# Down projection as seven half-size products over pairs of inner tiles, its operands staged in DRAM, with ScalarE's and VectorE's order written out by hand

## The chip, the cores and the metric

The kernel runs on one core of a Trainium2 chip. The metric is the device time of one execution in microseconds (us). Engines are named as in the profile: PE is TensorE's matmul, PEld its weight load, ACT ScalarE, DVE VectorE, POOL GpSimd, SP SyncE, which here only issues DMAs.

## What is computed

One step of an encoder layer over 640 tokens (512 of a prompt, 128 of running streams), model width 2048, inner width 5632, in fp32:

```python
def layer(x, lp, states):
...
    x = x + jnp.concatenate([y_a, y_b, y_c, y_d], axis=-1) @ w_out

    h = rmsnorm(x, g_ffn)
    gt, new_hist_f = causal_dwconv(h @ w_ffn_gate, ffn_conv_w, hist_f)
    x = x + (jax.nn.silu(gt) * (h @ w_ffn_up)) @ w_ffn_down
```

The four parts `y_a` to `y_d` (short convolution, gated linear attention, long convolution, banded attention) and the projections around them come first; the change touches what follows them, the last three lines. A final norm ends the step.

## The kernel before, in words

Activations lie transposed: features on the 128 partitions, the T = 640 tokens along the free axis, in two halves of H = 320. Width 2048 is KT = 16 tiles, the inner width NF = 44 tiles. An fp32 product is made of three matmuls in the reduced format fp32r: each operand is split into a high part (`hi`, a copy by ACT, L115) and a low part (`lo`, the difference, by DVE, L119), and hi·hi, hi·lo and lo·hi are added in PSUM. Weights come by SP's queue into `raw` (`wraw`, L101, three buffers) and are split by `wsplit` (L107). PE's order is the program's; DVE's and ACT's are set by a scheduler, with `high_priority` for some instructions.

**Gate and up** (L895 to L1013). A block of 256 inner columns by 2048 rows is one group `g` of 22, done first for the gate weights and then for the up weights. `seven` (L908) forms from the four blocks a11, a12, a21, a22 of the weights (each 128 x 1024) and from seven operand combinations `ops[0..6]` of the normed input, made once before, seven products of half size instead of eight: `product` (L895) is 8 x 3 = 24 matmuls of 128 weights by 320 columns. Sums of weight blocks are DVE adds of 128 x 1024 (L917, L923, L924, L929). `snap` (L903) copies a PSUM sum to SBUF on ACT, `put` (L946) combines a second sum with it on DVE. Gate results `fu` get the norm factor (L986, L987), the convolution of width 3 (L994 to L996) and a Silu (L998) to become `fc`; up results `ft` get the norm factor and are multiplied by `fc` (L1010 to L1012); POOL stores each inner tile `ft` to `td` in DRAM (L1013). POOL also copies the convolution's history to `hist` (L989, L990).

**Down projection** (L1016 to L1063). `act` (L1019) loads an inner tile of `td` to `ta` by SP and splits it. Five chunks of eight inner tiles follow: for each of the 16 output tiles, weights of 128 x 1024 are loaded (L1039, four rows of 1024 bytes per partition) and split, 48 matmuls run (`mm3`, L125), and DVE adds the sum to `acc` (L1046), which starts as the residual, read from `x1d`. The next chunk's inner tiles are loaded meanwhile. Inner tiles 40 and 41 follow with 192 matmuls, adds at L1060.

**Tail** (L1066 on). The last two inner tiles (weights `wl`), the final norm and the outputs.

A few lines say what the words can't:

```python
def mm3(ps, w, k, x, start, stop, m=P, halves=(0, 1)):
...
    for i, (a, j) in enumerate(((hi, 0), (hi, 1), (lo, 0))):
        for h in halves:
            PE.matmul(ps[:m, h, :H], a[:, k * m:(k + 1) * m], x[j][:, h * H:(h + 1) * H],
                      start=start and i == 0, stop=stop and i == 2)
```

## Time and profile before

| | us |
|---|---|
| median of 3 runs | 2719.23 |
| lowest run | 2717.56 |
| the profiled execution | 2721.07 |
| its span in the profile | 2719.3 |
| busy: PE | 2680.3 |
| busy: DVE | 1578.2 |
| busy: ACT | 913.2 |
| busy: POOL | 241.3 |

The profile shows one execution; times in it run from the span's start. Up to about 982 us the mixers and projections run, up to about 2067 gate and up, up to about 2671 the down projection, then the tail. Busy shares are averages over these stages. A row that counts matmuls gives their time in sequence on the chain of waits, while a row of one matmul gives its full length, of which the next one covers a part.

### The profile page before, as it was taken

The numbers are of one execution on the slowest core, as the hardware profiler recorded it, in microseconds if no ns is written. First come the engines' busy times: TensorE is split into PE (matmuls) and PEld (weight loads), VectorE is DVE, ScalarE is ACT, GpSimd is POOL, SyncE is SP. The second block draws the span as 40 slices with busy tenths as digits, with TensorE's granted clock in tenths as the row PEclk, the third lists the DMA queues.
The fourth block names the chain that finished last, engine by engine and source line by source line (L and its number), as shares of the span: only waits on it lengthen the run. The fifth ranks groups of instructions, "written<-read, shape, count | busy, mean of one in ns | idle before, by whom it ended". The sixth has DMA issues, their size and how long they took to land.

```text
span 2719.3 us, 42977 instructions
## 1 busy us (share of the span) xinstructions
PE 2680.3 (99%) x18156; PEld 2616.5 (96%) x18156; DVE 1578.2 (58%) x2248; ACT 913.2 (34%) x1243; POOL 241.3 (9%) x397
## 2 busy tenths in 40 slices
PE   8999999999999989999999999999999999999998
PEld 8988898999999989999999999999998999999997
DVE  6877434253533467777777877777776233242236
ACT  5113434331332344344444434434444122121113
POOL 0012110000000011111111111111111000000002
PEclk9999999999999989999999999999999999999999
DMA  6334332222243323333233233332237233232223
GB/s 217 89 111 127 108 94 66 83 72 63 78 133 119 112 76 99 108 98 101 94 102 111 91 100 100 105 99 94 97 113 256 75 112 113 78 104 78 73 76 117
DMA packets 118969, 281.42 MB, mean 103 GB/s; under 512 B 11192, under 2 KB 58968, under 8 KB 118776
## 3 DMA queue, kind: packets, MB, share of 16 engines
q1 hardware_dynamic: 107544, 241.26, 27.9%
q0 software_dynamic: 11088, 37.41, 4.2%
q8 instruction: 142, 2.33, 0.4%
q14 instruction: 51, 0.42, 0.1%
q10 hardware_dynamic: 144, 0.01, 0.0%
HBM read 248.93 MB, written 32.46 MB: 103 GB/s over the span
## 4 chain that ended last, share of the span: by engine, by line
PE 90%; issue 6%; DVE 2%; ACT 1%; DMA 1%; POOL 0%; SPq 0%; ACTq 0%; POOLq 0%; DVEq 0%
PE main L130 42%; PE b L900 40%; PE main L157 3%; PE m L157 1%; PE main L1083 1%; PE m L463 1%; PE m L442 1%; PE m L476 0%; DMA ta<-td 0%; PE main L745 0%; PE m L210 0%; DMA raw<-in_w_in 0%; PE m L199 0%; DVE lo L119 0%; DVE sq L226 0%
## 5 line engine op out<-in xcount | busy, mean ns | idle before, releaser
L130 PE MATMUL main<-o,hi 128*128 128x320 f32 x5888 | 1116.8, 312 | 13.2 <-ACT o L219 6.4
L900 PE MATMUL b<-op,hi 128*128 128x320 f32 x4928 | 1085.8, 309 | 11.0 <-ACT hi L115 9.8
L130 PEld LDWEIGHTS main<-o,hi 128*128 128x128 f32 x5888 | 926.4, 189 | 26.7 <-issue 7.4
L900 PEld LDWEIGHTS b<-op,hi 128*128 128x128 f32 x4928 | 825.5, 188 | 12.0 <-ACT hi L115 10.1
L900 PE MATMUL b<-op,lo 128*128 128x320 f32 x2464 | 762.6, 309 | 0.7 <-DVE lo L119 0.7
L115 ACT ACTIVATE hi<-raw 128x1024 fp32r<-128x1024 f32 (+1 forms) x337 | 356.3, 1057 | 1157.8 <-PE main L130 817.1
L130 PE MATMUL main<-o,lo 128*128 128x320 f32 x2944 | 674.2, 310 | 0.8 <-DVE lo L119 0.8
L119 DVE TENSOR_TENSOR lo<-raw,hi 128x1024 fp32r<-128x1024 f32 (+1 forms) x337 | 411.6, 1222 | 322.3 <-ACT hi L115 317.5
L130 PEld LDWEIGHTS main<-o,lo 128*128 128x128 f32 x2944 | 494.4, 189 | 1.3 <-DVE lo L119 1.3
L900 PEld LDWEIGHTS b<-op,lo 128*128 128x128 f32 x2464 | 463.6, 188 | 1.3 <-DVE lo L119 1.3
L1046 DVE TENSOR_TENSOR acc<-acc,main 128x640 f32<-128x640 f32 x80 | 65.7, 822 | 371.8 <-PE main L130 371.8
L119 DVE TENSOR_TENSOR lo<-x,hi 128x1024 fp32r<-128x1024 f32 x132 | 161.6, 1225 | 104.8 <-ACT hi L115 99.9
L115 ACT ACTIVATE hi<-x 128x1024 fp32r<-128x1024 f32 x132 | 139.9, 1060 | 224.7 <-PE b L900 214.1
L119 DVE TENSOR_TENSOR lo<-a,hi 128x1024 fp32r<-128x1024 f32 x44 | 54.0, 1227 | 97.8 <-ACT hi L115 97.8
L905 ACT ACTIVATE sn<-b 128x320 f32<-128x320 f32 x176 | 74.6, 424 | 92.1 <-PE b L900 92.1
L989 POOL COPY hist<-fu 128x2 f32<-128x2 f32 x44 | 79.5, 1806 | 119.0 <-DVE fu L986 118.8
L346 DVE SCALAR_TENSOR_TENSOR cc<-gp,pb,cc 128x512 f32<-128x512 f32 x120 | 89.7, 747 | 0.0
L157 PE MATMUL main<-hi,o 128*128 128x512 f32 x256 | 84.6, 391 | 0.0
L996 DVE SCALAR_TENSOR_TENSOR fc<-fu,pb,fc 128x656 f32<-128x656 f32 x88 | 79.0, 898 | 0.7
L115 ACT ACTIVATE hi<-a 128x1024 fp32r<-128x1024 f32 x44 | 46.6, 1060 | 79.7 <-PE b L900 46.8
L1013 POOL DMA_DIRECT2D td<-ft x44 | 23.8, 541 | 454.9 <-DVE ft L1012 437.1
L990 POOL COPY hist<-fu 128x16 f32<-128x16 f32 x44 | 31.1, 707 | 354.8 <-DVE fu L987 354.8
(291 smaller groups left out, 1804.0 us busy)
## 6 DMA issues: line engine op xcount, KB each, us to landing
raw<-in_w_d SPq DMA_DIRECT2D x88, 512.0 KB, 3.7
raw<-in_w_in SPq DMA_DIRECT2D x71, 512.0 KB, 3.8
raw<-in_w_g SPq DMA_DIRECT2D x66, 512.0 KB, 3.7
raw<-in_w_u SPq DMA_DIRECT2D x66, 512.0 KB, 3.9
td<-ft POOLq DMA_DIRECT2D x44, 320.0 KB, 2.5
ta<-td SPq DMA_DIRECT2D x44, 320.0 KB, 4.9
raw<-in_w_out SPq DMA_DIRECT2D x24, 512.0 KB, 3.8
a<-in_w_g SPq DMA_DIRECT2D x22, 512.0 KB, 3.7
```

The source lines that it names most:

```text
L115: S.activation(hi[:, c], raw[:, c], AF.Copy)
L119: latest[0] = V.tensor_sub(lo[:, c], raw[:, c], hi[:, c].bitcast(F32)).ins
L130: PE.matmul(ps[:m, h, :H], a[:, k * m:(k + 1) * m], x[j][:, h * H:(h + 1) * H], start=start and i == 0, stop=stop and i == 2)
L157: PE.matmul(pss[t], opnd[kt][j][:, t * P:(t + 1) * P], w[:, k * 512:(k + 1) * 512], start=(kt == 0 and i == 0), stop=(kt == KT - 1 and i = ...
L346: V.scalar_tensor_tensor(c[:, :512], gp[:, j:j + 512], w(j), c[:, :512], op0=ALU.mult, op1=ALU.add)
L442: PE.transpose(pp[:, t, :], p[:, t * P:(t + 1) * P], ident)
L900: PE.matmul(ps, a[:, kt * P:(kt + 1) * P], o[:, j, kt % 2], start=(start and kt == 0 and i == 0), stop=(kt == 7 and i == 2), skip_group_ch ...
L905: S.activation(t, ps, AF.Copy)
L989: G.tensor_copy(hist[:, k, 0:2], u[:, 512:514])
L990: G.tensor_copy(hist[:, k, 2:].rearrange("p (b t) -> p b t", b=NB), su(u)[:, :, 16:])
L996: V.scalar_tensor_tensor(c[:, :n], u[:, q:q + n], w[:, q:q + 1], c[:, :n], op0=ALU.mult, op1=ALU.add)
L1046: V.tensor_add(v2(acc[c]), v2(acc[c]), ps[:, :, :H])
```

## The change

The stages up to the output projection keep PE's order. In gate/up PE's products stay the same, 308 of 24 matmuls. What changes:

- ACT's and DVE's order is by hand: `run(q)` is one product slot. It issues ACT's high part of product q + 1, the product's matmuls, the lists `fronts` and `mids` of slot q, DVE's low part of q + 1, then the lists `sums` and `backs`. `after`, `put_in` and a table put work into these lists. `snap` is gone: `seed` copies a sum straight to its place in `fu` or `ft`, and `put` adds there.
- `stage` takes the two inner tiles of a group (a pair) and makes the seven operands of the down projection: four combinations by DVE and, for all seven, a high part by ACT and a low part by DVE, each then stored by POOL's queue to `od` in DRAM (320 KB a store). Pairs are made of inner tiles 4 to 41, 19 pairs. Inner tiles 0 to 3, 42 and 43 are only split and stored to `sd`.
- The down projection has a plain phase, inner tiles 0 to 3 for 16 output tiles, and then 32 steps. A step takes two output tiles (m of 8) and a run of pairs (four rounds, widths from `BOUNDS`), and makes seven products of width x 3 matmuls. Weights come by SP in rows of 512 bytes, a block per tag and one buffer each, their sums `x1`, `x2` are DVE adds, and `gather` adds each product's sum to `acc`.
- Pairs come back from `od` by POOL's queue (`fetch_pair`, three loads of 640 KB and one of 320 KB). Seven stay in SBUF; the next is fetched when the steps that are left no longer need the oldest. The residual comes by ACT's queue.
- The weights' pools move to the other side of SBUF; the tail's own are opened after the steps.

```diff
+od = drp.tile([19, P, 7, 2, H], F32, name="od")
+sd = drp.tile([6, P, 2, T], F32, name="sd")
...
-def seven(src, after=()):
-    after = dict(after)
-    a11, a21, a22 = wraw(src[0][:, :1024]), wraw(src[1][:, :1024]), wraw(src[1][:, 1024:])
-    with tc.high_priority():
-        a12 = gw.tile([P, 1024], F32, tag="r2", name=nm("a12"))
-        Y.dma_start(a12, src[0][:, 1024:])
-        x = gw.tile([P, 1024], F32, tag="xs", name=nm("x"))
-        V.tensor_add(x, a21, a22)
-    a, c, e, d = (bank8()[:, :H] for _ in range(4))
-    product(0, a, wsplit(a11))
-    p1 = snap(a)
-    w = wsplit(x)
-    with tc.high_priority():
-        V.tensor_add(x, x, a11)
-        V.tensor_add(a21, a21, a11)
-    product(4, c, w)
-    p5 = snap(c)
...
+TAKES = ("a11", "x", "x", "a22", "a21", "a12", "x")
+USES = (0, 4, 5, 3, 6, 1, 2)
...
+def hi_of(q):
+    if q < NQ:
+        v, i = divmod(q, 7)
+        src = raws[v][TAKES[i]]
+        hi = wp.tile([P, 1024], F32R, tag="hi", name=nm("hi"))
+        lo = wp.tile([P, 1024], F32R, tag="lo", name=nm("lo"))
+        S.activation(hi, src, AF.Copy)
+        wq[q] = hi, lo, lambda: V.tensor_sub(lo, src, hi.bitcast(F32))
+def lo_of(q):
+    if q < NQ:
+        wq[q][2]()
...
+    def seed(i, ps):
+        for c, o in dst[i]:
+            S.activation(o, piece(ps, c, o), AF.Copy)
...
+    after(0, seed, 0)
+    after(1, seed, 3)
+    after(2, seed, 1)
+    after(4, seed, 2)
+    after(4, put, 3)
+    sums[q + 5].append(lambda: put(2, bk["e"]))
+    after(5, put, 0)
+    after(6, put, 1)
+    for n, f in ((0, lambda: wadd(v, "x", "x", "a11")), (2, lambda: wadd(v, "a21", "a21", "a11")),
+                 (2, lambda: wload7(v + 1, "a11", "a22")), (3, lambda: wadd(v, "x", "x", "a12")),
+                 (3, lambda: wload7(v + 1, "a21")), (4, lambda: wload7(v + 1, "a12")),
+                 (6, lambda: wadd(v + 1, "x", "a21", "a22", True))):
+        sums[q + n].append(f)
...
+    hi_of(q + 1)
+    product(USES[i], bk[banks[i]], wq.pop(q), i not in (2, 4, 6))
+    for f in fronts[q] + mids[q]:
+        f()
+    lo_of(q + 1)
+    for f in sums[q] + backs[q]:
+        f()
...
+def split_to(src, place):
+    o = slot([P, 2, H], F32R, n="sp")
+    S.activation(o[:, 0], src, AF.Copy)
+    V.tensor_sub(o[:, 1], src, o[:, 0].bitcast(F32))
+    G.dma_start(place, o.bitcast(F32))
+def stage(g, ts):
+    b11, b12, b21, b22 = (t[:, h * H:(h + 1) * H] for t in ts for h in range(2))
+    if g < 2 or g == 21:
+        for j in range(2):
+            for h in range(2):
+                split_to(ts[j][:, h * H:(h + 1) * H], sd[(2 * g if g < 2 else 4) + j, :, :, h * H:(h + 1) * H])
+                yield
+        return
+    place = od[g - 2]
+    o1, o2, o3, o4 = (slot([P, 2, H], F32R, n="op") for _ in range(4))
+    f1, f2, f3, f4 = (o[:, 1].bitcast(F32) for o in (o1, o2, o3, o4))
+    def parted(i, o, f):
+        S.activation(o[:, 0], f, AF.Copy)
+        V.tensor_sub(o[:, 1], f, o[:, 0].bitcast(F32))
+        G.dma_start(place[:, i], o.bitcast(F32))
+    V.tensor_sub(f1, b11, b12)
+    V.scalar_tensor_tensor(f2, f1, -1.0, b22, op0=ALU.mult, op1=ALU.subtract)
+    yield
+    V.scalar_tensor_tensor(f3, f2, -1.0, b21, op0=ALU.mult, op1=ALU.subtract)
+    V.tensor_sub(f4, b22, b12)
+    yield
+    for i, (o, f) in enumerate(((o1, f1), (o2, f2), (o3, f3))):
+        parted(i + 1, o, f)
+        yield
+    for src, i in ((b11, 0), (b21, 5), (b22, 6)):
+        split_to(src, place[:, i])
+        yield
+    parted(4, o4, f4)
...
+    for i, f, a, into in (
+            (8, normed, (1,), mids), (8, conv, (1, 0), backs), (8, normed, (0,), backs),
+            (9, conv, (1, 1), mids), (9, conv, (0, 0), backs), (10, conv, (1, 2), mids),
...
+            (17, staging, (), mids), (17, more, (), mids), (18, more, (), mids),
...
+        put_in(i, f, *a, into=into)
...
-def act(f, pool=opp):
-    t = slot([P, T], n="ta")
-    Y.dma_start(t, td[f])
-    o = pool.tile([P, 2, T], F32R, tag="o", name=nm("o"))
-    S.activation(o[:, 0], t, AF.Copy)
-    V.tensor_sub(o[:, 1], t, o[:, 0].bitcast(F32))
-    return o[:, 0], o[:, 1]
...
-for ch in range(5):
-    cur, nxt = nxt, []
-    for c in range(KT):
-        with tc.high_priority():
-            raw = wp.tile([P, 1024], F32, tag="raw", name=nm("raw"), bufs=3)
-            Y.dma_start(raw.rearrange("p (g k) -> p g k", g=4),
-                        A["w_d"][4 * ch:4 * ch + 4, :, c * 256:(c + 1) * 256].rearrange("g p k -> p g k"))
-        w = wsplit(raw)
-        ps = mtile()
-        for i in range(8):
-            mm3(ps, w, i, cur[i], i == 0, i == 7)
-        with tc.high_priority():
-            V.tensor_add(v2(acc[c]), v2(acc[c]), ps[:, :, :H])
-        if c % 2 == 0 and ch < 4:
-            nxt.append(act(8 * ch + 8 + c // 2))
...
+BOUNDS = ((2, 7, 13, 19), (3, 8, 14, 19), (4, 9, 14, 19), (4, 9, 14, 19),
+          (5, 10, 14, 19), (5, 10, 14, 19), (5, 11, 15, 19), (6, 12, 15, 19))
+steps = [(m, BOUNDS[m][r - 1] if r else 0, BOUNDS[m][r]) for r in range(4) for m in range(8)]
...
+def down_raw(tag, c, n, g0, g1, j=None):
+    t = wtile(tag)
+    k = slice(c * 256, (c + 1) * 256) if j is None else slice(c * 256 + j * P, c * 256 + (j + 1) * P)
+    with tc.high_priority():
+        Y.dma_start(t[:, :n].rearrange("p (g k) -> p g k", g=g1 - g0),
+                    A["w_d"][g0:g1, :, k].rearrange("g p k -> p g k"))
+    return t
...
+    cur, acc = [plain(f, G) for f in range(4)], []
...
+def fetch_pair(p):
+    got = []
+    for i in range(3):
+        d = nd[0] % 21
+        nd[0] += 1
+        o = (opp if d < 16 else opp2 if d < 20 else xpd).tile([P, 2, 2, H], F32R, tag="o", name=nm("b"))
+        G.dma_start(o.bitcast(F32), od[p, :, 2 * i:2 * i + 2])
+        got += [o[:, 0], o[:, 1]]
+    o = xps.tile([P, 2, H], F32R, tag="o", name=nm("b"))
+    G.dma_start(o.bitcast(F32), od[p, :, 6])
+    pairs[p] = got + [o]
+with tc.manual_schedule(engines={mybir.EngineType.Pool}):
+    for p in range(7):
+        if p in (0, 3):
+            G.tensor_copy(gate, acc[2 * p][:, :1])
+        fetch_pair(p)
...
+    for s, (m, lo, hi) in enumerate(steps):
+        r0, r1 = acc[2 * m], acc[2 * m + 1]
+        both = r1.rearrange("p (h n) -> p h n", h=2)
+        a, c, e, d = (bank8()[:, :H] for _ in range(4))
+        def times(i, ps, start=True):
+            w = ws.pop(7 * s + i)
+            for p in range(lo, hi):
+                o, k = pairs[p][i], slice((p - lo) * P, (p - lo + 1) * P)
+                for q, (x, j) in enumerate(((w[0], 0), (w[0], 1), (w[1], 0))):
+                    PE.matmul(ps, x[:, k], o[:, j], start=(start and p == lo and q == 0),
+                              stop=(p == hi - 1 and q == 2), skip_group_check=not start)
+        def gather(op, out, ps):
+            op(out, out, ps)
+        q = 7 * s + 2
+        hi_down(q)
+        times(0, a)
+        late()
+        lo_down(q)
+        add(s, "x1", "a21", "a11")
+        hi_down(q + 1)
+        times(1, c)
+        gather(V.tensor_add, r0[:, :H], a)
+        lo_down(q + 1)
+        add(s, "x2", "x2", "a12", False)
+        load(s + 1, "a21", "a11", "a22")
+        hi_down(q + 2)
+        times(2, a, False)
+        gather(V.tensor_sub, r1[:, H:], c)
+        lo_down(q + 2)
+        hi_down(q + 3)
+        times(3, e)
+        gather(V.tensor_add, r0[:, H:], a)
+        lo_down(q + 3)
+        load(s + 1, "a12")
+        hi_down(q + 4)
+        times(4, a, False)
+        gather(V.tensor_sub, r1[:, :H], e)
+        lo_down(q + 4)
+        add(s + 1, "x1", "a21", "a22")
+        hi_down(q + 5)
+        times(5, d)
+        gather(V.tensor_sub, both, a[:, None, :].to_broadcast([P, 2, H]))
+        lo_down(q + 5)
+        hi_down(q + 6)
+        times(6, c, False)
+        gather(V.tensor_add, r0[:, :H], d)
+        add(s + 1, "x2", "x1", "a11")
+        lo_down(q + 6)
+        def late(r0=r0, c=c):
+            gather(V.tensor_add, r0[:, H:], c)
+        free = min([HB] + [x for _, x, _ in steps[s + 1:]])
+        while done < free:
+            if done + 7 < HB:
+                fetch_pair(done + 7)
+            done += 1
```

**The start of gate/up on DVE.** Before, in two pieces; `op` are operand forms of the normed input, `x_1124` to `x_1127` the last output tiles, `lo_9037` the low part of product 0, `lo_9067` that of the next:

```order
L119 TENSOR_TENSOR lo_8896<-raw_8892,hi_8895 128x1024
L119 TENSOR_TENSOR lo_9037<-raw_9022,hi_9036 128x1024
L816 TENSOR_TENSOR x_1124_8499<-x_1124_8499,main_8495 128x640
L816 TENSOR_TENSOR x_1125_8501<-x_1125_8501,main_8496 128x640
L226 TENSOR_TENSOR sq_1000_7131<-sq_1000_7131,sq_1152_8949 128x640
```

```order
L830 TENSOR_TENSOR op_8992<-r_8971,op_8992 128x640
L830 TENSOR_TENSOR op_8995<-q_8972,op_8995 128x640
L917 TENSOR_TENSOR x_9030<-raw_9024,raw_9026 128x1024
L830 TENSOR_TENSOR op_8998<-x_1126_8503,op_8998 128x320
L924 TENSOR_TENSOR raw_9024<-raw_9024,raw_9022 128x1024
L119 TENSOR_TENSOR lo_9067<-x_9030,hi_9066 128x1024
```

After, from the same form on; `lo_9032` is the low part of product 0:

```order
L835 TENSOR_TENSOR op_8998<-r_8977,op_8998 128x640
L835 TENSOR_TENSOR op_9001<-q_8978,op_9001 128x640
L932 TENSOR_TENSOR x_9029<-raw_9023,raw_9025 128x1024
L941 TENSOR_TENSOR lo_9032<-raw_9021,hi_9031 128x1024
L835 TENSOR_TENSOR op_9004<-x_1126_8509,op_9004 128x320
L835 TENSOR_TENSOR op_9004<-x_1127_8511,op_9004 128x320
L835 TENSOR_TENSOR op_9009<-x_1126_8509,op_9009 128x320
L835 TENSOR_TENSOR op_9009<-x_1127_8511,op_9009 128x320
L941 TENSOR_TENSOR lo_9049<-x_9029,hi_9048 128x1024
```

The low part of product 0 has moved from ahead of the output tiles' adds to behind the last combined form and the add of `x`; the four remaining forms stand between it and the next product's low part.

**Gate/up in the staged groups on ACT.** Before, the first slots' neighbours in a group (`hi` the high parts, `sn` the snaps):

```order
L905 ACTIVATE sn_16213<-b_16118 128x320 [waits PE_49]
L115 ACTIVATE hi_16279<-a_2056_16114 128x1024 [waits DMAHW0_49,PE_49,Activation_49]
L115 ACTIVATE hi_16308<-x_16116 128x1024 [waits DVE_49,PE_49]
L905 ACTIVATE sn_16271<-b_16118 128x320 [waits PE_49]
L115 ACTIVATE hi_16361<-raw_16347 128x1024 [waits DMAHW1_49,DVE_49,PE_49]
L115 ACTIVATE hi_16391<-x_16355 128x1024 [waits DVE_49,PE_49,Activation_49]
```

After, in the slots in which the pair of the group before is staged (`op` a combination, `sp` a block that is only split, `fu` a seed):

```order
L940 ACTIVATE hi_18883<-x_18695 128x1024 [waits DVE_49,PE_49,Activation_49]
L954 ACTIVATE fu_18700<-b_18703 128x320 [waits PE_49]
L1023 ACTIVATE op_18837<-op_18837 128x320 [waits DVE_49]
L1004 ACTIVATE sp_18918<-ft_18447 128x320 [waits DMASW1_49,DVE_49]
L940 ACTIVATE hi_18922<-raw_18802 128x1024 [waits DMAHW5_49,PE_49]
L1004 ACTIVATE sp_18953<-ft_18448 128x320 [waits DMASW2_49,DVE_49]
L940 ACTIVATE hi_18963<-x_18951 128x1024 [waits DVE_49,PE_49,Activation_49]
```

Splits of staged operands now stand between the high parts of the products, and they wait for DMAs, the stores of what was in their buffer.

**The down projection on DVE.** Before, in a chunk:

```order
L1046 TENSOR_TENSOR acc_19805<-acc_19805,main_21113 128x640
L119 TENSOR_TENSOR lo_21227<-raw_21224,hi_21226 128x1024
L1046 TENSOR_TENSOR acc_19805<-acc_19805,main_21174 128x640
L119 TENSOR_TENSOR lo_21288<-raw_21285,hi_21287 128x1024
L1046 TENSOR_TENSOR acc_19808<-acc_19808,main_21230 128x640
```

After, in the first step, width 2 (`x_2609` is `x1`, `x_2568` `x2`, `acc_20243` the first two output tiles):

```order
L1153 TENSOR_TENSOR lo_2608_20919<-x_2568_20802,hi_2607_20918 128x256
L1181 TENSOR_TENSOR x_2609_20928<-a_2556_20730,a_2551_20696 128x256
L1309 TENSOR_TENSOR acc_20243<-acc_20243,b_20914 128x320
L1153 TENSOR_TENSOR lo_2611_20931<-a_2561_20764,hi_2610_20930 128x256
L1181 TENSOR_TENSOR x_2568_20802<-x_2568_20802,a_2566_20798 128x256
L1309 TENSOR_TENSOR acc_20243<-acc_20243,b_20915 128x320
L1153 TENSOR_TENSOR lo_2616_20949<-x_2609_20928,hi_2615_20948 128x256
L1309 TENSOR_TENSOR acc_20243<-acc_20243,b_20914 128x320
L1153 TENSOR_TENSOR lo_2618_20960<-a_2566_20798,hi_2617_20959 128x256
L1309 TENSOR_TENSOR acc_20243<-acc_20243,b_20916 128x320
```

A low part and an add of 640 per 48 matmuls have become low parts, sums of weights and gathers for each product of 6 matmuls in this step.

## Rows read from the trace of the kernel before

**Rows 1.** The page's first part: busy us, share, instructions of each engine.
```profile
PE 2680.3 (99%) x18156; PEld 2616.5 (96%) x18156; DVE 1578.2 (58%) x2248; ACT 913.2 (34%) x1243; POOL 241.3 (9%) x397
```

**Rows 2.** Windows by stage: length, busy us (instructions) by engine, clock, DMA share, GB/s.
```profile
982.00:2064.00 1082.00, 1081.32 (x7361) 1080.23 (x7362) 814.45 (x1012) 446.95 (x574) 148.16 (x224) 1.00 0.32 104
...
2081.00:2671.00 590.00, 590.00 (x4005) 589.64 (x4005) 210.00 (x221) 117.51 (x124) 0.00 (x0) 1.00 0.30 96
```

**Rows 3.** Chain of waits: start us, us, what held it.
```profile
1001.67 1058.46 PE b L900 x7223
...
2073.78 5.98 DMA ta<-td
2080.57 590.20 PE main L130 x4002
2670.77 16.89 PE main L1083 x96
```

**Rows 4.** Finer windows from gate/up to down projection.
```profile
2045.00:2064.00 19.00, 19.00 (x132) 19.00 (x131) 14.00 (x17) 9.06 (x13) 4.96 (x3) 1.00 0.97 330
...
2072.00:2076.00 4.00, 3.52 (x15) 3.53 (x16) 2.07 (x3) 1.43 (x3) 0.52 (x1) 0.64 0.77 255
2076.00:2081.00 5.00, 2.39 (x10) 1.47 (x9) 1.27 (x2) 1.69 (x3) 0.00 (x0) 0.84 1.00 353
```

**Rows 5.** TensorE's timeline, end of gate/up: start us, us, line, operation.
```profile
2066.99 0.31 PE L900 MATMUL b<-op,lo 128*128 128x320 f32 x1
```

**Rows 6.** VectorE's groups in gate/up: busy us, mean ns, idle before.
```profile
L119 DVE TENSOR_TENSOR lo<-x,hi 128x1024 fp32r<-128x1024 f32 x132 | 161.6, 1225 | 104.8 <-ACT hi L115 99.9
...
L1010 DVE TENSOR_TENSOR ft<-ft,rstd 128x640 f32<-128x640 f32 x43 | 35.4, 822 | 0.8
...
L1011 DVE TENSOR_TENSOR ft<-ft,fc 128x512 f32<-128x512 f32 x42 | 28.7, 683 | 0.0
L950 DVE SCALAR_TENSOR_TENSOR ft<-b,sn 128x320 f32<-128x320 f32 x44 | 21.2, 483 | 0.0
...
L950 DVE SCALAR_TENSOR_TENSOR fu<-b,sn 128x192 f32<-128x192 f32 x22 | 7.7, 350 | 0.0
```

**Rows 7.** ScalarE's groups in gate/up, same columns.
```profile
L115 ACT ACTIVATE hi<-x 128x1024 fp32r<-128x1024 f32 x131 | 138.8, 1060 | 224.0 <-PE b L900 214.1 <-DVE x L923 9.9
L905 ACT ACTIVATE sn<-b 128x320 f32<-128x320 f32 x175 | 74.2, 424 | 92.1 <-PE b L900 92.1
```

**Rows 8.** TensorE's waits: engine, line, waited for: total us, times, longest.
```profile
PE b L900 <- ACT hi L115: 9.8, 1, 9.8
```

**Rows 9.** Windows at the start of gate/up.
```profile
972.00:982.00 10.00, 0.17 (x3) 0.02 (x1) 8.34 (x13) 6.25 (x11) 1.63 (x4) 0.60 0.10 28
982.00:988.00 6.00, 5.32 (x19) 4.92 (x20) 5.65 (x8) 1.06 (x1) 0.00 (x0) 0.52 0.34 119
```

**Rows 10.** VectorE's timeline at the start of gate/up.
```profile
978.89 0.82 DVE L830 TENSOR_TENSOR op<-q,op 128x640 fp32r<-128x640 f32 x1
979.62 1.22 DVE L917 TENSOR_TENSOR x<-raw,raw 128x1024 f32<-128x1024 f32 x1
...
982.29 1.22 DVE L119 TENSOR_TENSOR lo<-x,hi 128x1024 fp32r<-128x1024 f32 x1
```

**Rows 11.** The page's DMA issues: count, KB each, median us to landing.
```profile
raw<-in_w_d SPq DMA_DIRECT2D x88, 512.0 KB, 3.7
...
raw<-in_w_g SPq DMA_DIRECT2D x66, 512.0 KB, 3.7
...
ta<-td SPq DMA_DIRECT2D x44, 320.0 KB, 4.9
```

**Rows 12.** The tile td: its DMAs.
```profile
DMA to landing us min/median/max: 2.4/3.1/7.0
```

**Rows 13.** The page's groups: GpSimd's DMA issues of td.
```profile
L1013 POOL DMA_DIRECT2D td<-ft x44 | 23.8, 541 | 454.9 <-DVE ft L1012 437.1
```

More of the change, by code (lines that the diff above doesn't have):

```diff
@@ L952, in encoder_kernel @@
         rstd2 = rstd
-        box = {}
+        plan = []
         def stat1():
@@ L963, in stat2 @@
             S.activation(rstd2[:, 512:], p1[:, :TS], AF.Copy)
+        full = slice(0, H)
         for g in range(22):
[L966 to L976 removed]
@@ L1000, in encoder_kernel @@
[L1000 to L1013 removed]
+            q0 = 14 * g
@@ new lines, in scaled, with gated, staging, more @@
+            def scaled(j, ts=ts):
+                V.tensor_mul(ts[j], ts[j], rstd2)
+            def gated(j, ts=ts, cs=cs):
+                V.tensor_mul(ts[j][:, :512], ts[j][:, :512], cs[j][:, :512])
+                V.tensor_mul(sa(ts[j]), sa(ts[j]), su(cs[j])[:, :, :16])
+            def staging(g=g, ts=ts):
+                box["stage", g] = stage(g, ts)
+            def more(g=g):
+                next(box["stage", g], None)
+            def put_in(i, f, *args, into=backs):
+                into[q0 + i].append(lambda: f(*args))
@@ new lines, in encoder_kernel @@
+            plan.append((begin, dst, begin_up))
+        HB, WN = 19, 768
+        TAGS = ("a11", "a21", "a22", "a12")
+        BOUNDS = ((2, 7, 13, 19), (3, 8, 14, 19), (4, 9, 14, 19), (4, 9, 14, 19),
+                  (5, 10, 14, 19), (5, 10, 14, 19), (5, 11, 15, 19), (6, 12, 15, 19))
+        steps = [(m, BOUNDS[m][r - 1] if r else 0, BOUNDS[m][r]) for r in range(4) for m in range(8)]
+        raw = [{} for _ in steps]
+        TAKES_D = ("a11", "x1", "x2", "a22", "x1", "a12", "x2")
+        ws, plain_raw = {}, {}
@@ new lines, in load, with load_plain, add @@
+        def load(s, *names):
+            if s < len(steps):
+                m, lo, hi = steps[s]
+                for n in names:
+                    raw[s][n] = down_raw(n, 2 * m + (n[1] == "2"), (hi - lo) * P, 2 + lo, 2 + hi, int(n[2] == "2"))
+        def load_plain(c):
+            if c < KT:
+                plain_raw[c] = down_raw(TAGS[c % 4], c, 512, 0, 2)
+            elif c < KT + 4:
+                load(0, TAGS[c - KT])
+        def add(s, out, x, y, new=True):
+            if s < len(steps):
+                n = (steps[s][2] - steps[s][1]) * P
+                if new:
+                    raw[s][out] = wtile(out)
+                V.tensor_add(raw[s][out][:, :n], raw[s][x][:, :n], raw[s][y][:, :n])
@@ new lines, in hi_down, with lo_down, plain @@
+        def hi_down(q):
+            s, i = divmod(q, 7)
+            if q < 0:
+                parts(q, plain_raw[q + KT], 512, box.pop("hl", None))
+            elif s < len(steps):
+                parts(q, raw[s][TAKES_D[i]], (steps[s][2] - steps[s][1]) * P)
+        def lo_down(q):
+            if q in ws:
+                ws[q][2]()
+        def plain(f, q):
+            o = opp2.tile([P, 2, T], F32R, tag="o", name=nm("a"))
+            q.dma_start(o.bitcast(F32), sd[f])
+            return o[:, 0], o[:, 1]
@@ new lines, in encoder_kernel @@
+        with tc.manual_schedule(engines={mybir.EngineType.Pool}):
[3 more added lines that the diff above has]
+                fetch_pair(p)
+        with tc.manual_schedule(engines={mybir.EngineType.Activation, mybir.EngineType.DVE}):
+            done, late = 0, lambda: None
+            for s, (m, lo, hi) in enumerate(steps):
[53 more added lines that the diff above has]
+                    done += 1
+                if s == 28:
+                    prev = [plain(4 + j, Y) for j in range(2)]
+            late()
```

284 lines of the change are left out of this document (179 added, 105 removed).

## Prediction

> **What bounds the kernel now.** The page's first part is read first: TensorE is busy 99% of the span [rows 1]. The windows by stage then show where this holds: in gate/up TensorE is busy 1081.3 of 1082 us at granted clock 1.00, in the down projection 590.0 of 590.0 [rows 2]; VectorE has 814.5 us there, 75%, and then 210.0, 36%. So matmul count sets both stages, and a removed matmul comes off the end as long as no other engine or transfer takes its place. The chain of waits gives the price: 7223 gate/up matmuls in 1058.46 us, 146.5 ns each, and 4002 down matmuls in 590.20 us, 147.5 ns [rows 3]. Between the stages is a hole: the chain goes through loads of `ta` and the down matmuls begin at 2080.57 [rows 3]. Finer windows show the DMA engines full there (0.97, 330 GB/s before the hole, 1.00 and 353 GB/s in it) and the clock at 0.64 and 0.84 [rows 4].
>
> The profiled execution took 2721.07 us (span 2719.3 and 1.77 around it); the median is 1.84 lower. The sum is made on 2721.07 and 1.84 taken off at the end. Two per cent, about what a measurement of this kernel can tell from no change, lies at 2664.9 and 2773.6.
>
> **The down projection: what goes.** Before, 4032 matmuls of 128x320 stand between the end of gate/up's last matmul, which starts at 2066.99 and gives way at about 2067.2 [rows 5], and the tail's first at 2670.77 [rows 3]: 603.5 us. By the code the new count is 16 x 24 = 384 in the plain phase and 152 pair-steps x 7 x 3 = 3192 in the 32 steps, 3576 in all, each on the same 128 rows and 320 columns: 456 fewer. At 146.5 ns that is 523.9 us. The saving is 66.8 us of matmuls and some 12.8 us of the hole and its slow clock: the new order loads the four plain operand tiles and the first weights within the last gate/up group, so the hole has nothing left to wait for. At 147.5 ns the stage would be 3.6 us longer.
>
> **Gate/up: what is added.** 7392 matmuls as before. VectorE does 37.0 us of work per group of 14 products (814.45 / 22), and a group lasts 14 x 24 x 0.1465 = 49.2 us. Staging adds four operand combinations and seven low parts, eleven instructions of 128x320 at 0.484 us, 5.3 us [rows 6]: 42.3 of 49.2, 86%. ScalarE gets seven copies of 0.424 us [rows 7] on 446.95 / 22 = 20.3 us per group, 48%. Both stay under TensorE's time, so the steady state costs nothing as a sum; what can cost is order, since both engines now go by lists. By the lists the next product's low part stands behind at most about 2.8 us of a slot of 3.52 us, so I put 1 us on it for the whole stage (0 to 15: a twentieth of a us per product).
>
> At the start there is a loss. Before, the low part of product 0 was made ahead of the operand forming, and its matmuls ran in the gaps; TensorE then waited 9.8 us for the next high part [rows 8], at a clock that falls to 0.60 and 0.52 [rows 9]. Now that low part stands behind the last combined form and an add. Before, the form at 978.89 and the add at 979.62 are followed by the next low part at 982.29 [rows 10]; now product 0 itself starts at about 982. One product more is left, 24 x 0.1465 = 3.5 us, partly under the same slow stretch: +3 (1 to 7, the upper end being the product at half clock).
>
> **The down steps: what is added.** Each step makes seven high and low parts, four adds and seven gathers for VectorE, against 7 products of 3 matmuls, 21 per pair. Of width 4: 7 low parts and 4 adds of 512 columns at 0.683, six gathers at 0.484 and one of 640 at 0.822 [rows 6], 11.2 us, against 84 matmuls, 12.3 us. Width 6: some 14.2 against 18.5. Only the two narrow steps that come first go the other way: width 2, with 256 columns at about 0.42 (between 0.350 for 192 and 0.484 for 320), 8.3 against 6.2; width 3, 9.8 against 9.2. That is 2.7 us, and with the latency of their weight loads I take +4 (2 to 9).
>
> Weights of the next step are loaded while this one runs. At width 4 the first-needed low part of the next step allows some 5 to 6 us, at width 5 and 6 up to 10; before, a weight load lands in 3.7 us, whether it has 512 rows of 1024 bytes (down) or 128 rows of 4096 (gate/up) [rows 11]. The new rows are 512 bytes, which no row here shows. Below, they cost as bytes do, and then 256 KB land sooner than 512 KB did: nothing is lost. Above, a row of 512 costs like one of 1024 and each burst of a pair (2.24 MB, 6.8 us at 330 GB/s) holds the loads behind it: some 2 us per step, 64 us. I take +4, near the lower end, since the two row lengths that the trace has cost the same, and since the stage as a whole asks for about 46 MB of weights and 43.6 MB of pairs in 524 us, 171 GB/s, half of the 330 that is seen. The Trainium skill, "DMA: Bandwidth & Descriptors", Specifications, puts the least transfer for full rate at 512 bytes, so by it these loads lose nothing; no run here shows it, and by it this term would be 0 instead of 4.
>
> The tail's code is the same, but its weight splits stand behind the last gather, which waits for the last product: +2 (0 to 5).
>
> **Sum.** 2721.07 - 603.5 + 523.9 + 3 = 2644.5; with 1 + 4 + 4 + 2 for order, first steps, loads and tail 2655.5; less 1.84, 2653.
>
> **Rivals.** (a) The steps wait for transfers. Pairs are fetched in bursts, weights come in short rows on another queue, and the hole of before shows what full DMA engines do: there a load of 320 KB takes 4.9 us [rows 11] and TensorE's clock falls. One us per step is 32 us, 2685; two are 2717. Against it stands the average of 171 GB/s. Chance 0.16.
>
> (b) VectorE paces gate/up. It is at 86% with an order that can't move a ready instruction ahead. The gain of 68 us is gone at 0.22 us per product (308 products). At a third of that, 2676; chance 0.07.
>
> (c) The stores land late: the slower side. Of the operands staged, the first goes to DRAM by GpSimd's queue at the end of the fifth product slot of the next gate product; ScalarE's next split takes a buffer only when that store has landed, and behind this split stands the high part of a later product. By the lists TensorE waits when landing takes over 7.03 us (two slots) + 0.5 - 1.06 - 1.225 (high and low part, 1.225 as in rows 6 and 1.06 as in rows 7), about 5.3. Each us above costs 1 us in each of 19 groups. Before, the same size lands in 2.4, 3.1 and 7.0 us (least, middle, most) [rows 12], and an issue costs GpSimd 0.541 us [rows 13]; two a group there, seven now, in bursts. The gain is gone at 5.3 + 68 / 19 = 8.9 us, and slower by 2% begins at 11.8, where each group loses 6.5. From there on it decides; the middle of 3.1 speaks against it. Chance 0.07, of which 0.04 slower: 2780 at 12 us.
> The Trainium skill, "SBUF — State Buffer", The single rule, speaks against this move: a DMA issued from GpSimd's queue needs descriptors that GpSimd writes, and VectorE can hold the port they share for a whole instruction. The trace has such stores beside a VectorE 75% busy, and half of them land within 3.1 us, so it shows no hold of more than an instruction or so. If each store lost one instruction of 1.225 us, the middle would be 4.3, still under 5.3, and the forecast stands; by the rule the chance of (c) is a little higher, and is put so.
>
> **How the numbers follow.** Forecast 0.70, between 2640 and 2665; (a) 0.16; (b) 0.07; (c) 0.07. Faster by over 2% needs less than 2664.9: the forecast, and a little of (a) and (b), 0.72. Within 2%: the rest of (a) and (b) and the mild half of (c), 0.24. Slower 0.04. The low end is the sum without any stall and a start of +1: 2641 - 1.84 = 2640, and another 3 where the slow stretch at the start goes, 2637. The high end takes in (a) at a little over 1 us per step: 2690.
>
> **What would show it.** Right: 3576 down matmuls at about 147 ns, TensorE busy all but some 10 us between the last gate/up matmul and the tail; no hole and no fall of the clock between the stages; VectorE at 84 to 88% in gate/up; od stores landing in 3 to 4 us. The steps of width 2 and 3 lose a few us to VectorE and nothing later does. Wrong: TensorE waiting for a low part by some tenths of a us in most products (b); for the high part behind a split, once in each group (c); for `x1` or `a12` of the next step in most steps, with the DMA share near 1 in those stretches (a).

## The result, and the profile after

The changed kernel takes 2673.26 us in the median (2670.79 to 2676.59, four runs), the kernel before 2719.23 beside it: a ratio of 0.9831, 95% interval 0.9812 to 0.985. A fourth run of the kernel before, of 4390.88 us, is slow and stands in neither number. The change is faster by 46 us where 66 were forecast. The time lies in the range, but the gain is 1.7%, which falls in the case "within 2%" that had a chance of 0.24 against 0.72 for more.

The profiled execution took 2676.59 us, the longest of the four and 21.1 more than the 2655.5 of the sum. Counted at fixed matmuls of the two traces, the terms came out so (us):

| term | forecast | measured | read from |
|---|---|---|---|
| up to gate/up's first matmul | 0 | +7.7 | 974.19 against 966.49 |
| start of gate/up | +3 | +2.3 | its 500th matmul, 10.0 later, less 7.7 |
| rest of gate/up | +1 | +7.8 | its last matmul, 2084.79 against 2066.99, less 10.0 |
| down projection, 3576 matmuls | 523.9 | 524.7 | 538.4 less what is lost in steps |
| lost in steps | +8 | +13.7 | 10.5, 0.9 and 0.2 in steps 0 to 2, 2.1 in step 24 |
| tail | +2 | +2.8 | 51.5 against 48.7 to the end |

The page's first part, after, to be held against [rows 1]:

```profile
PE 2624.7 (98%) x17700; PEld 2555.8 (96%) x17700; DVE 1867.7 (70%) x2869; ACT 1013.0 (38%) x1544; POOL 323.4 (12%) x580
```

The windows by stage, after (length, busy us and instructions of PE, PEld, DVE, ACT, POOL, clock, DMA share, GB/s): gate/up, the plain phase, the first step, the other steps.

```profile
988.00:2085.00 1097.00, 1093.03 (x7405) 1088.48 (x7406) 921.31 (x1234) 498.05 (x762) 187.52 (x327) 1.00 0.38 130
2085.00:2141.00 56.00, 56.00 (x383) 55.88 (x382) 26.32 (x53) 11.22 (x20) 15.77 (x30) 1.00 1.02 380
2141.00:2158.00 17.00, 9.08 (x46) 8.81 (x45) 8.84 (x22) 3.79 (x9) 2.25 (x5) 0.70 0.83 308
2158.00:2623.30 465.30, 462.96 (x3152) 462.22 (x3151) 366.65 (x558) 158.43 (x218) 25.52 (x48) 1.00 0.50 149
```

Against [rows 2], VectorE is busy 84% in gate/up, as worked out. The hole of [rows 4] between the stages is gone. The DMA engines are full there still, at 380 GB/s, and TensorE's hole has moved 56 us on, into the first step: the clock of 0.70 there is a stretch of 10.2 us at half clock (granted 0.50, 1.2 GHz) in 17. TensorE's waits and its timeline say for what (start, us, operation, and in brackets the idle time before it):

```profile
PE b L905 <- DVE lo L941: 16.9, 5, 15.1
PE b L1305 <- DVE lo L1153: 9.7, 2, 7.9
```

```profile
1216.53 0.41 PE L905 MATMUL b<-op,lo 128*128 128x320 f32 x1 [0.37 <-DVE lo L941]
...
1615.51 0.42 PE L905 MATMUL b<-op,lo 128*128 128x320 f32 x1 [0.70 <-DVE lo L941]
...
2149.77 0.64 PE L1305 MATMUL b<-b,lo 128*128 128x320 f32 x1 [7.92 <-DVE lo L1153]
...
2503.41 0.41 PE L1305 MATMUL b<-b,lo 128*128 128x320 f32 x1 [1.81 <-DVE lo L1153]
```

The 15.1 us at the start stand where 9.8 stood [rows 8]. The rest are short waits in some staged groups, one of 7.92 us in step 0, and one of 1.81 us in step 24. Behind these stand DMAs. Below are the chain of waits to the second of these lines, the page's issues (KB each, us to landing), the stores' own view, and two loads from the chain to step 0:

```profile
1606.36 6.33 DMA od<-op
...
1612.78 0.04 ACT sp L1004
...
1613.15 1.05 ACT hi L940
...
1614.23 1.24 DVE lo L941
...
1615.51 4.57 PE b L905 x29
```

```profile
b<-od POOLq DMA_DIRECT2D x57, 640.0 KB, 6.5
...
od<-op POOLq DMA_DIRECT2D x76, 320.0 KB, 4.3
a<-in_w_d SPq DMA_DIRECT2D x64, 320.0 KB, 4.0
od<-sp POOLq DMA_DIRECT2D x57, 320.0 KB, 2.4
```

```profile
  ACT sp L1004: 45.9, 17
...
DMA to landing us min/median/max: 2.4/4.3/6.6
```

```profile
2118.18 15.09 DMA a<-in_w_d
2134.76 12.85 DMA a<-in_w_d
```

`od<-op` lands in 4.3 us where `od<-sp`, as large and by the same queue, lands in 2.4, and ScalarE's split `sp` waited for it 17 times. The 4.3 is a median over four stores a pair: the first two take 4.2 to 6.6 us (medians 4.6 and 4.8), the third and fourth 2.45 in the median. The weights of the plain phase's 15th output tile took 15.09 us to land, and a block of step 0's 12.85; the four blocks of step 0 took 12.5 to 15.1.

### The profile page after: what moved, and what is told of

The parts are those of the page before. It is cut to its first block, busy times and chain, and to the rows that moved or that the text cites. A ratio compares the mean times of both kernels' runs of the same rounds, so it can differ in the third digit from the quotient of the medians.

```text
span 2674.8 us, 43731 instructions
## 1 busy us (share of the span) xinstructions
PE 2624.7 (98%) x17700; PEld 2555.8 (96%) x17700; DVE 1867.7 (70%) x2869; ACT 1013.0 (38%) x1544; POOL 323.4 (12%) x580
## 4 chain that ended last, share of the span: by engine, by line
PE 78%; issue 14%; DMA 4%; DVE 3%; POOL 1%; ACT 1%; SPq 0%; ACTq 0%; DVEq 0%; POOLq 0%
PE b L905 30%; PE main L132 21%; PE b L1305 16%; PE main L159 3%; DMA a<-in_w_d 2%; DMA od<-op 1%; PE b L1243 1%; PE m L159 1%; PE main L1386 1%; PE m L466 1%; PE m L445 1%; PE m L479 0%; POOL hist L1085 0%; ACT hi L940 0%; PE main L748 0%
## 5 line engine op out<-in xcount | busy, mean ns | idle before, releaser
L132 PE MATMUL main<-o,hi 128*128 128x320 f32 x3200 | 611.2, 313 | 7.6 <-ACT o L222 6.7
L132 PEld LDWEIGHTS main<-o,hi 128*128 128x128 f32 x3200 | 505.4, 190 | 18.8 <-issue 7.5
L905 PEld LDWEIGHTS b<-op,lo 128*128 128x128 f32 x2464 | 464.3, 188 | 21.1 <-DVE lo L941 20.6
L1305 PE MATMUL b<-b,hi 128*128 128x320 f32 x2128 | 470.4, 310 | 0.5 <-DVE acc L1309 0.5
L132 PE MATMUL main<-o,lo 128*128 128x320 f32 x1600 | 367.3, 311 | 0.8 <-DVE lo L121 0.8
L1305 PEld LDWEIGHTS b<-b,hi 128*128 128x128 f32 x2128 | 357.3, 189 | 0.9 <-issue 0.9
L1305 PE MATMUL b<-b,lo 128*128 128x320 f32 x1064 | 329.5, 310 | 9.7 <-DVE lo L1153 9.7
L121 DVE TENSOR_TENSOR lo<-raw,hi 128x1024 fp32r<-128x1024 f32 (+1 forms) x121 | 147.1, 1215 | 262.1 <-ACT hi L117 256.4
L117 ACT ACTIVATE hi<-raw 128x1024 fp32r<-128x1024 f32 (+1 forms) x121 | 127.1, 1051 | 476.8 <-PE main L132 375.1
L132 PEld LDWEIGHTS main<-o,lo 128*128 128x128 f32 x1600 | 270.3, 190 | 1.3 <-DVE lo L121 1.3
L1305 PEld LDWEIGHTS b<-b,lo 128*128 128x128 f32 x1064 | 201.3, 189 | 10.3 <-DVE lo L1153 10.3
```

The costliest lines, as they stand in the source:

```text
L117: S.activation(hi[:, c], raw[:, c], AF.Copy)
L121: latest[0] = V.tensor_sub(lo[:, c], raw[:, c], hi[:, c].bitcast(F32)).ins
L905: PE.matmul(ps, a[:, kt * P:(kt + 1) * P], o[:, j, kt % 2], start=(start and kt == 0 and i == 0), stop=(kt == 7 and i == 2), skip_group_ch ...
L1305: PE.matmul(ps, x[:, k], o[:, j], start=(start and p == lo and q == 0), stop=(p == hi - 1 and q == 2), skip_group_check=not start)
```

## The experiments

**The change once more.** No edit.

> The changed kernel once more, for its first 980 us. Its profiled execution reached the first gate/up matmul 7.7 us later than the kernel before (974.19 against 966.49), with the same order on every engine up to there, and with two stretches of 3.4 us at half clock near 544 and 633 us that the kernel before doesn't have. If that is the one execution, this profile begins gate/up within 4 us of 966.5 and has no such stretches, or has them elsewhere. If it comes of the moved pools, it begins near 974 again. Median 2671 to 2676 either way.

2672.42 us, ratio to the kernel before 0.9825 (0.9811 to 0.984). Gate/up began at 971.62, with one stretch at half clock, near 630. So the 7.7 us are part chance, part not: every profile of the change and its variants lies between 969.7 and 974.2.

**The splits one slot later.**

```diff
-(18, more, (), backs), (18, more, (), backs), (19, more, (), backs), (19, more, (), backs),
-(20, more, (), backs), (21, more, (), backs), (22, more, (), backs)):
+(18, more, (), backs), (18, more, (), backs), (19, more, (), backs), (20, more, (), backs),
+(21, more, (), backs), (22, more, (), backs), (23, more, (), backs)):
```

> The four last staging pieces of a group one product slot later, so that ScalarE's first plain split asks for its buffer 3.5 us later; nothing else changes. Theory (the store of the first operand lands in 4.2 to 6.3 us, the split waits for it, and all above about 4.5 us is lost in each of 19 groups): the 1500th to the 4500th gate/up matmul take 439.5 us as in the kernel before instead of 445.6, no wait of TensorE for a low part after the start, and the median falls by 6 to 8 us, to 2665 to 2667. Rival (VectorE's load of 85% and its fixed order lose the time): the sum of work is the same, so 445 us and 2673 stay.

2669.56 us, 0.9814 (0.9799 to 0.9828). From the 1500th to the 4500th gate/up matmul it took 440.2 us (the change 445.6, the kernel before 439.5). Of TensorE's waits for a low part in gate/up only that at the start is left:

```profile
PE b L905 <- DVE lo L941: 15.2, 1, 15.2
```

That stretch alone would not settle it: in the repeat of the change it took 442.4. From the 500th matmul to the last, the change's profile and its repeat took 1017.6 and 1016.4, the run with the later load below, whose schedule came out as the change's, 1018.6, and this run 1011.2. What the first stores of the pairs took over 4.6 us each adds up to 6.4, 5.1 and 7.4 in those three: the same 6.4, 5.2 and 7.4 us. Here the first stores land as late (4.2 to 6.3 us), VectorE has the same work in nearly the same order, and the time is gone: rival (c) is what gate/up lost. Only 3 or 4 of the 6 us show in the median, whose runs overlap the repeat's; in this profile steps 0 and 1 lost 14.2 us instead of 11.4.

The run shows one thing more. The fourth combination's store went with the split, and is now issued 0.67 us behind a load of 512 KB by SP (in 17 of 19 pairs). It lands in 5.3 us in the median, where it took 2.45 in the change, and nothing waits for it. The same store by the same queue is late where a load was issued just ahead of it.

**One store more.**

```diff
+        spare = drp.tile([19, P, 2, H], F32, name="spare")
...
+                if i == 1:
+                    G.dma_start(spare[g - 2], o.bitcast(F32))
                 G.dma_start(place[:, i], o.bitcast(F32))
```

> The first operand of each pair is stored to a second, unused place in DRAM just ahead of its own store, so that its own lands later by 320 KB more in the same burst; the output is the same. Theory (the split waits for this store, and what it lands over 4.5 us is lost): it lands at about 6 to 6.5 us instead of 4.2 to 6.3, each of 19 groups loses 1.3 to 2 us more, and gate/up grows by 20 to 35 us over the changed kernel's 1110.6; the median is 2693 to 2708. Rival (VectorE's load): no VectorE work is added, so gate/up grows by under 5.

2685.52 us, 0.9862 (0.9848 to 0.9876). Gate/up, first matmul to last, grew from 1110.6 to 1121.0: 10.4 us, 0.55 per group, half of what was expected and over the rival's 5. The direction is the theory's, the size is not: the store is issued 0.53 us later and lands 0.8 us behind the extra one, 1.6 us behind SP's load instead of 0.8. 320 KB more ahead of it did not add the 2.4 us that they take alone. In the change a group whose first store lands in 4.3 us lasts 49.3 us, with 5.2 some 49.9, with 6.3 it is 51.0: all above 4.6 is lost, one for one.

**The load beside the stores, later.**

```diff
-(4, lambda: wload7(v + 1, "a12")),
+(5, lambda: wload7(v + 1, "a12")),
```

> The weight block a12 of the next product set is loaded one product slot later, so that SP's load of 512 KB no longer starts 0.6 us ahead of the first two stores of a pair; splits, stores and queues as in the change. Theory (those two stores land in 4.2 to 6.3 us, where all others land in 2.4, since they share the DMA engines with that load): they land in 2.4 to 3.2 us, no wait of TensorE in the staged groups, gate/up from its 500th matmul to its last 1011 us as in the run with the later split, instead of 1016 to 1017.6, and a median 4 to 7 us lower. Rival (GpSimd's queue is late because VectorE holds the port it needs, or two stores in a row are slow in themselves): they land in 4 us or more again and nothing changes.

2675.35 us, 0.9826 (0.981 to 0.9843). The load did not move: it still starts 0.67 us ahead of the first store, so its place in the program is not what it waits for. The run tells nothing of the theory, and its expected gain did not come; it is the change measured a third time.

**The stores by SP's queue.**

```diff
-                G.dma_start(place[:, i], o.bitcast(F32))
+                Y.dma_start(place[:, i], o.bitcast(F32))
```

> The four combinations of each pair are stored by SP's queue instead of GpSimd's; all else is the same. Theory (the load beside them is what they wait for): the first two still land in 4 us or more. Rival (descriptors that GpSimd writes while VectorE holds the shared port): they land in about 2.4 us. In both cases SP's weight loads stand behind stores that wait for VectorE, which may cost gate/up some us of its own; the time is only looked at: 2665 to 2690.

A single run, 2674.46 us. The first store of a pair lands in 4.8 to 6.3 us, median 4.95, issued 0.40 us after the load where GpSimd's was issued 0.67 after it. So GpSimd's queue is not what makes it late, and no hold of the shared port by VectorE (the Trainium skill, "SBUF — State Buffer", Who interferes with whom, the single rule) is seen in these stores; that section tells of it for VectorE's two-port modes, which it says `tensor_tensor` lacks. What the runs show is one distance: in 18 of the change's 19 pairs the store lands 0.77 to 0.85 us after SP's load of 512 KB that was issued 0.67 us ahead of it, whether that load took 4.1 or 6.2 us, and with SP's queue 0.78 to 0.86. This store lands behind the load issued ahead of it, on the other queue too. The Trainium skill, "DMA: Bandwidth & Descriptors", Issuing engines are not separate DMA queues, says that all of them run on the same 16 engines; the runs agree.

**The last four pairs later.**

```diff
-                if p in (0, 3):
-                    G.tensor_copy(gate, acc[2 * p][:, :1])
+                if p in (0, 3, 4):
+                    G.tensor_copy(gate, acc[{0: 0, 3: 12, 4: 15}[p]][:, :1])
```

> The fourth pair is fetched after the plain phase's 13th output tile, the three after it after the 16th, instead of all four after the 7th. Theory (the fetches fill the DMA engines at 382 to 398 GB/s from 2100 to 2150, the first step's weights take 13 to 15 us to land, TensorE waits 7.9 us and runs at half clock for 10.2 us): the first step takes 6 to 9 us instead of 16.7, its weights land in 5 to 9 us, the clock stays, and the median falls by 8 to 11 us, to 2662 to 2665. Rival (the narrow first steps are VectorE's, 8.3 us against 6.15, or rows of 512 bytes are slow): the first step still takes over 12 us and the median falls by under 4.

2678.39 us, 0.9844 (0.9828 to 0.9861), 6 us slower than the change's repeat, and all its four runs lie above all of the repeat's. Step 0 lost 1.2 us instead of 10.5, as the theory has it, and step 1 lost 14.5: the burst had moved onto the next step's weights, two blocks of which took 15.0 and 18.5 us to land. Windows and timeline of this run:

```profile
2148.00:2160.00 12.00, 0.67 (x2) 0.67 (x3) 2.48 (x5) 0.52 (x1) 1.61 (x3) 0.63 1.03 396
```

```profile
2159.33 0.64 PE L1305 MATMUL b<-b,lo 128*128 128x320 f32 x1 [11.66 <-DVE lo L1153]
```

TensorE stands still at whichever step has its weights behind the burst, with the DMA engines full (396 GB/s). The gain expected in the median was wrong, the mechanism is what the run shows.

**The pairs one by one.**

```diff
-            for p in range(7):
+            for p in range(4):
                 if p in (0, 3):
-                    G.tensor_copy(gate, acc[2 * p][:, :1])
+                    G.tensor_copy(gate, acc[4 * p][:, :1])
...
+                if s in (1, 3, 5):
+                    G.tensor_copy(gate, r0[:, :1])
+                    fetch_pair(4 + s // 2)
```

> Pairs 0 to 2 as they were, pair 3 after the plain phase's 13th output tile, pairs 4, 5 and 6 one each after steps 1, 3 and 5. Theory (it is the burst of pairs that holds the next step's weights, wherever it stands: 10.5 and 0.9 us lost in steps 0 and 1 as the change has it, 1.2 and 14.5 when the burst stood later): no burst is over 2.24 MB, steps 0, 1 and 2 lose under 5 us together instead of 11.5, and the median falls by 6 to 10 us, to 2663 to 2667. Rival (narrow steps with rows of 512 bytes can't be fed in any order): they lose 10 or more again.

2669.43 us, 0.9809 (0.9795 to 0.9822). Steps 0 to 2 lost 2.0 us, so narrow steps and rows of 512 bytes can be fed. But steps 3 and 9 lost 3.7 and 3.9, each with 3.4 us at half clock: even one or two pairs, fetched just ahead of the next step's weights, make them land in 6.4 to 8.4 us for step 3 and in 8.2 to 11.5 for step 9.

**The first low part early.**

```diff
+        with tc.high_priority():
+            wload7(0, "a11", "a21", "a22", "a12")
+            hi_of(0)
+            lo_of(0)
+            wadd(0, "x", "a21", "a22", True)
         with tc.manual_schedule(engines={mybir.EngineType.Activation, mybir.EngineType.DVE}):
-            with tc.high_priority():
-                wload7(0, "a11", "a21", "a22", "a12")
-                wadd(0, "x", "a21", "a22", True)
-                hi_of(0)
-                lo_of(0)
```

> The first product's high and low parts are made in the scheduled part of the program, ahead of the operand forming, as in the kernel before. Theory (one product more is left when the last form is done): the first product runs in the gaps again, the 500th gate/up matmul comes 2 to 3 us earlier against the first, and the median falls by 1 to 3 us, to 2670 to 2672. Rival (the slow clock after the 15 us gap is what costs, and a product in the gaps does not shorten it): less than 1 us.

2673.08 us, 0.983 (0.9816 to 0.9845). The 500th gate/up matmul came 90.3 us after the first, against 93.0 and 93.2 in the two profiles of the change: 2.8 us, as expected. The median does not show it; in this profile the rest of gate/up, from that matmul on, took 1020.1 us against 1017.6 and 1016.4.

**The weights' pool moved, alone.** In the kernel before:

```diff
-        wp = ctx.enter_context(tc.tile_pool(name="wp", bufs=2))
+        wp = ctx.enter_context(tc.tile_pool(name="wp", bufs=2, side="right"))
```

> The kernel before, with the weights' pool on the other side of SBUF and nothing else. Five profiles of the change show the matmuls of 512 columns whose moving operand is a weight (output of 128 tokens by 512) at 234.3 ns each between 117 and 180 us, the kernel before 226.8; and one or two stretches of 3.4 us at half clock near 543 and 630 us, the kernel before none. If the place of the pool is the reason, this kernel shows 234.3, and with it 1.7 us more at its 1000th matmul; if not, 226.8. The stretches at half clock come along only if they hang on it too. Median 2719 to 2726.

2726.35 us over ten runs, 1.0018 (1.0009 to 1.0027): the move alone costs some 4.6 us (2.4 to 7.3). In its one profile gate/up begins at 970.19, 3.7 us later than before. Twelve matmuls of 512 columns in the chain of the kernel before, and of this one:

```profile
176.52 2.72 PE main L157 x12
```

```profile
175.57 2.80 PE main L157 x12
```

The stretches at half clock did not come along: there is none before 970 us in either.

**The pool aligned.** In the changed kernel:

```diff
+        padp = ctx.enter_context(tc.tile_pool(name="padp", bufs=1, side="right"))
+        padp.tile([P, 24], F32, name="pad")
         wp = wp_ctx.enter_context(tc.tile_pool(name="wp", bufs=2, side="right"))
```

> 96 bytes of padding per partition ahead of the weights' pool, so that its tiles begin at a multiple of 128 bytes as in the kernel before, instead of 96 bytes past one; nothing else. Theory (the matmuls of 512 columns whose moving operand is a weight run at 234.3 ns instead of 226.8 since their moving operand starts off such a multiple): they take 226.8 again, and the 1000th matmul comes 1.7 us earlier against the 700th; the median falls by 1 to 4 us. Rival (the place of the pool as such, on the upper side of SBUF): 234 again, no change.

2667.37 us, 0.9802 (0.9788 to 0.9817). The same twelve matmuls in the change and here:

```profile
176.22 2.81 PE main L159 x12
```

```profile
174.51 2.75 PE main L161 x12
```

From the 700th to the 1000th matmul the change takes 63.1 us, this run 61.9, the kernel before 61.5. 96 bytes of address are worth most of that, not all; the 226.8 ns that were expected did not come. The median is 5 to 8 us under the three of the change, more than these matmuls account for, and where the rest comes from is not shown; one stretch at half clock is here too.

**Three edits, and all of them.** The splits later, the low part early, the pairs one by one:

> The three edits together: the splits a slot later, the first product's low part early, the pairs one by one. If the three losses are separate they add: 6 us of gate/up, 2.8 of the start and 6 to 9 of the steps, some 16 us, a median of 2655 to 2660. If they share one cause further down (the same transfers late elsewhere), less than half of that comes off, and the median stays above 2665.

2661.24 us, 0.9781 (0.9768 to 0.9795): 12 us off, between the two cases; in its profile gate/up takes 1101.9 us instead of 1110.6 and the steps lose 9.0 instead of 14.3. The last run adds the padding and fetches single pairs in the middle of steps:

```diff
                 gather(V.tensor_sub, r1[:, :H], e)
+                if s in (2, 4, 6, 8):
+                    G.tensor_copy(gate, r1[:, :1])
+                    fetch_pair(3 + s // 2 if s < 8 else 8)
+                    done += s == 8
                 lo_down(q + 4)
...
-                while done < free:
+                while done < free and (s, done) != (7, 1):
```

> The three edits, the padding, and pairs 4, 5, 6 and 8 fetched in the middle of steps 2, 4, 6 and 8, behind the loads of the next step's weights instead of ahead of them. Theory (a burst of one pair ahead of those loads still cost 2 us in step 3 and 2 in step 9): steps 3 and 9 lose under 0.5 us, the matmuls of 512 columns take 226.8 ns, and the median falls by 4 to 7 us from the run with three edits, to 2654 to 2658. Rival (those steps wait for something else): 2660 and over.

2654.67 us, 0.9756 (0.9741 to 0.9771), 67 us under the kernel before and 19 under the change. Its gate/up and first two steps by windows:

```profile
988.00:2072.00 1084.00, 1084.00 (x7377) 1083.52 (x7376) 916.60 (x1227) 498.80 (x760) 177.38 (x327) 1.00 0.38 132
2072.00:2128.50 56.50, 56.50 (x387) 56.50 (x386) 28.46 (x59) 11.86 (x21) 11.64 (x22) 1.00 0.92 331
2128.50:2144.00 15.50, 14.25 (x94) 13.48 (x93) 14.08 (x32) 6.24 (x13) 0.00 (x0) 1.00 0.41 117
```

Step 3 loses nothing now, but steps 9 and 10 lost 0.9 and 4.0 us: pairs 8 and 9 are fetched one right after the other, and step 10's weights took 11.7 to 12.6 us to land. The median is as expected, these steps are not. The matmuls of 512 columns take 227.6 and 231.6 ns, not 226.8.

## Why the prediction was right, and where it was wrong

The mechanism of the gain is right: matmuls that are gone came off the end. The forecast of 2640 to 2665 that had 0.70 was missed all the same. The sum, 2653, is 20 us too low, no errors cancel to speak of, and the time lies in the stated range since its upper end took in rival (a). The low end has a slip that changes nothing: the sum without stalls and with a start of +1 is 2642.5, less 1.84 2640.6.

- **The matmuls.** 456 fewer at 146.5 ns, and the hole gone: right, to 0.8 us. The work was where the profile put it.
- **The start.** +3 against +2.3, and the run that put the low part ahead took 2.8 back: right.
- **Gate/up.** VectorE at 86% costs nothing as a sum: right (84%, and the same load without waits once the splits stand later). "I put 1 us on it for the whole stage" failed: it was 7.8. The later splits took 6.4 of it back; the rest is open. The mechanism was in the text as rival (c), but its threshold was put at 5.3 us (its terms add up to 5.2) where it is 4.6, and the landing was taken from the spread of `td` [rows 12], whose middle is 3.1. That row counts the 44 stores and the 44 loads that bring `td` back; the stores alone have a middle of 2.5 (this view is of their line, L1013):

```profile
DMA to landing us min/median/max: 2.4/2.5/5.8
```

Of these stores all but two are issued over 4.7 us after SP's last load. The new first stores are issued 0.67 us behind a load of 512 KB, every time. The kernel before had one such case, a store 1.1 us behind a load: it took 3.5 us and landed 0.84 us behind it. The sign named for (c) was wrong too: TensorE waits for the low part, which the text gave to (b), because the high part that the split holds up comes before it in the chain.

- **The first steps and the loads.** +4 and +4 against 13.7, with the place wrong. The loss was spread over 32 steps, from an average of 171 GB/s; 28 of them lose 0.03 us or less in the change's profile. What costs 11.6 of the 13.7 is the one burst of seven pairs, 15.7 MB, beside residual and weights: "171 GB/s, half of the 330 that is seen" is an average over a stage that starts at 380. Rival (a) has the right cause and the wrong price, per step instead of per burst. VectorE's 2.7 us for the two narrow steps could not be seen beside that; with the pairs one by one these steps lost 0.5 and 1.5, VectorE busy 9.98 of the 10.69 us of step 1. Step 24 lost 1.2 to 2.2 us in every profile, against "nothing later does": it is 6 wide and follows a third narrow step, which the text did not count, so its weights, 384 KB a block, are issued 4 to 7 us before it starts; no run tests this. Rows of 512 bytes cost little: 320 KB in such rows, with no other load beside them, took 3.2 us, where 512 KB in rows of 1024 take 3.7 [rows 11]. Whether they go at the full rate that the Trainium skill, "DMA: Bandwidth & Descriptors", Specifications, puts at 512 bytes and over, these runs don't tell.
- **Before gate/up.** Costed at nothing without a word, since PE's order there is the same: it was 3.2 to 7.7 us in all profiles. The moved pool is a part of it, shown by the kernel before with that edit alone. One or two stretches of 3.4 us at half clock, in a TensorE that the profile shows busy, come with every profile of the change and its variants; the kernel before has none, nor has it with the pool moved. Each stretch begins 2.2 to 3.3 us after the start of a run of twenty matmuls of one column (the `osq` sums of squares); the first of the change's two:

```profile
540.52 2.29 PE L202 MATMUL m<-one,osq 128*128 128x1 f32 x20
```

```profile
543.80:547.20 3.40, 3.40 (x15) 3.40 (x15) 2.85 (x8) 1.66 (x2) 0.00 (x0) 0.50 0.46 154
```

The kernel before has the same two runs of twenty, and in the change only 13 of 24 are followed by a stretch, so whether the change brings the stretches or chance does stays open.

- **The tail.** +2 against +2.8, and +1.5 in the repeat's profile, which lacks a stretch of 3.4 us at half clock that this one has near 2660.

The chances were too sure of a gain over 2%: two of the three costs that were missed stood in the text as rivals, at 0.16 and 0.07, and a part of each came at once; the third, before gate/up, stood nowhere.

## What to carry to other kernels

Ask of a DMA not how long it takes in the median row but what is issued just ahead of it, on any queue; and ask of such a row what it counts. Ask of a stage not its mean GB/s but what its first microseconds fetch; split a prefetch into pieces and put each behind the loads that are needed sooner. A pool that is moved is an edit: give it a term.

## What the runs showed of the hardware that was not expected

- A store of 320 KB lands 0.8 us after the load of 512 KB that was issued 0.67 us ahead of it on another queue, whatever that load takes (4.1 to 6.2 us), in 18 of the change's 19 pairs. One store more between the two put it 0.8 us further back. A store of the same size that took 2.45 us took 5.3 once it was issued 0.67 us behind such a load; it landed 0.75 to 0.85 us behind the load in 10 of 17 pairs, and between 0.4 us ahead of it and 0.4 us behind in the others.
- Matmuls of 512 fp32r columns, between 117 and 180 us, follow each other at 226.8 ns where the kernel before has the pool of their moving operand, at 234.3 in the change with the pool moved, at 234.5 (high part) and 231.0 (low part) in the kernel before with the pool moved, and at 227.6 (high part) and 231.6 (low part) after 96 bytes of padding. Those of 320 columns take 146.5 to 147 in all four. Why is not settled.
- The DMA engines moved 398 GB/s over 30 us of the change (2120 to 2150), above the 353 seen before.
